# Recurrence gates as 64-row matmuls of two heads in turn, and the convolution and split of u by halves of the tokens

## The chip, the core and the metric

The kernel runs on one core of one Trainium2 chip. Its engines, as the profile names them, are PE (TensorE: matmuls, with their weight loads shown apart as PEld), DVE (VectorE), ACT (ScalarE), POOL (GpSimd) and SP (SyncE, which issues the DMAs). Each runs its own instructions in order and waits on semaphores for the others. The metric is device time in microseconds (us) for one execution of the whole kernel, as a median over executions.

## The reference, cut to what matters

One encoder block on x of 1024 tokens by 1024 channels, in float32. A combined projection gives u, a gate g, attention inputs q, k, v and two merge gates. The change touches the recurrent mixer only:

```
uc = centred_depthwise_conv(u, conv_w, conv_b)        # 4 taps over tokens: t-2 .. t+1
h_fwd = rg_lru(uc, lam[0], wa[0], ba[0], wx[0], bx[0], False)
h_bwd = rg_lru(uc, lam[1], wa[1], ba[1], wx[1], bx[1], True)
y_a = (h_fwd + h_bwd) * gelu(g)

def rg_lru(u, lam, wa, ba, wx, bx, reverse):
    ub = u.reshape(bsz, s, 16, 64)                    # 16 heads of 64 channels
    r = sigmoid(einsum("bshi,hij->bshj", ub, wa) + ba)
    i = sigmoid(einsum("bshi,hij->bshj", ub, wx) + bx)
    log_a = -8 * r * softplus(-lam)
    a = exp(log_a);  beta = sqrt(max(-expm1(2 * log_a), 0))
    h = scan(h[t] = a[t] * h[t-1] + beta[t] * i[t] * u[t])   # over the tokens
```

`wa` and `wx` are 64x64 for each head and direction. Windowed attention (mixer B), the merge sigmoid(zA) * y_a + sigmoid(zB) * y_b, the product with w_out, and a SwiGLU follow; the change leaves them alone.

## The kernel before, in words

**Layout and precision.** Channels lie on the 128 partitions and the 1024 tokens along the row. Each float32 operand of a product is split into a high and a low part of TensorE's 32-bit matmul type: a copy to the rounded type (`to_hi`) and a subtraction (`to_lo`, L127). Each product then takes three matmuls: high x high, high weight x low data, low weight x high data. `xh`, `xl` are the normalised x; `whi`, `wlo` a weight block of 1024 rows by 128 columns, in a ring of three; their raw block `wraw` comes by DMA into a ring of two.

**Stages.** The kernel starts up, runs attention (to about 404 us), then a loop over eight chunks c = 0 to 7 of 128 channels for the recurrence (to about 690 us), then the product with w_out (`wo`) in two halves, then the SwiGLU.

**One chunk of the recurrence.** `token_product` makes the products u, g and za (the merge gate), each 48 matmuls: two halves n of 512 tokens, eight blocks k of the contraction, three matmuls for each. u goes into a PSUM tile `pu` of 1024 columns, of which there is one; g and za go through `pa`, two PSUM tiles of 512 columns in turn, which `evac_g` (gelu, into `gg`) and `evac_za` (tanh, into `sA`) empty on ScalarE. From the third chunk on the order is u, g, za; for the first two it is g0, za0, u0, g1, u1, za1.

When both halves of u are there, `evac_u` makes the convolution: one ScalarE operation over 1024 tokens (L599) and three on VectorE that add the other taps (L603), all reading `pu` and writing `uc`. Then `lru_chunk` is started. It fetches the heads' weights into `graw`, whose four 128x128 blocks (`wa`, `wx`, each for directions d = 0 and 1) hold two 64x64 heads on the diagonal and zeros elsewhere (L729 clears it once), splits them into `gh` (ScalarE) and `gl` (GpSimd), splits `uc` into `uh` (ScalarE, L120) and `ul` (VectorE, L127), and runs the gates: for each of four blocks a PSUM tile `gp` (two in turn), six matmuls, and one sigmoid of 128x1024 (L659) into `r` or `i`. Then come, for the two directions: tanh (L671) and a maximum (L672) into `q`, `i` times `uc` (L673), exp (L678), sqrt (L681), `q` times (1 + a) (L684), `i` times `q` (L685), and the scan (L687, L689). Their sum (L690) is multiplied by `gg` (L694) and added to the attention's result `y` (L695). ScalarE loads a table whenever it changes to a function of another set (the ACT_TABLE_LOAD rows).

**What sets the order.** TensorE's order is the order in which the code issues it. `clock` is a running estimate: `mm` adds 0.00042 us for each column, so 0.215 for 512. `lru_chunk` is a generator: each `yield` puts it into the heap `waiting` with a due time that many us ahead, and between two steps of the products `run_due` resumes what is due. So the numbers after `yield` place the four gate blocks between the projections' matmuls; `drain` at the end runs what is left. The other engines' order is chosen by the compiler's scheduler from its own estimates; `tc.high_priority` moves an operation ahead, `tc.issue_after(x)` keeps it behind x. Each engine then works strictly in that order. Buffers are rings too: `uc`, `gg` and `sA` share four (`qutile`), `uh` has two, `pu` one.

**Weights.** `weight(key)` hands out the block for a product and first fetches and splits all blocks up to two further along. `prep` says on which engine: GpSimd for both parts during the recurrence; ScalarE for the high part after `prep["hi"] = "act"`, which stands in front of the last `drain`. The first `wo` block is asked for at L861.

Of the kernel before, what the change touches and what calls it, by code (L numbers as in the profile page):

```python
# [16 lines left out]
P = 128  # L17
# [6 lines left out]
HD = 64  # L24
# [7 lines left out]
def kernel(  # L32
# [190 lines left out]
    def cb(c):  # L223
        return pv[:, 64 + c:65 + c]

    def gb(t, d, c):
        o = (88, 104)[t] + d * KD + c
        return pv[:, o:o + 1]

    stat = const.tile([P, 4 * NT], F32, name="stat")  # L230
    rstd = const.tile([P, 3 * NT], F32, name="rstd")
# [136 lines left out]

    def softplus():

        lam = pv[:, 72:88]
        e, z, z2, po = lt
        act.activation(e, lam, AF.Abs)
        act.activation(e, e, AF.Exp, scale=-1.0)
        dve.tensor_scalar(out=z, in0=e, scalar1=2.0, scalar2=None, op0=ALU.add)
        dve.reciprocal(z, z)
        dve.tensor_tensor(out=z, in0=z, in1=e, op=ALU.mult)
        dve.tensor_tensor(out=z2, in0=z, in1=z, op=ALU.mult)
        dve.tensor_scalar(out=po, in0=z2, scalar1=1.0 / 17.0, scalar2=None, op0=ALU.mult)
        for n in (15, 13, 11, 9, 7, 5, 3):  # L380
            dve.scalar_tensor_tensor(out=po, in0=po, scalar=1.0 / n, in1=z2, op0=ALU.add, op1=ALU.mult)
        dve.scalar_tensor_tensor(out=po, in0=po, scalar=1.0, in1=z, op0=ALU.add, op1=ALU.mult)
        dve.tensor_scalar(out=e, in0=lam, scalar1=-1.0, scalar2=0.0, op0=ALU.mult, op1=ALU.max)
        dve.scalar_tensor_tensor(out=e, in0=po, scalar=2.0, in1=e, op0=ALU.mult, op1=ALU.add)
        dve.tensor_scalar(out=sp4, in0=e, scalar1=0.5 * C_RG, scalar2=None, op0=ALU.mult)
        dve.tensor_scalar(out=spm8, in0=e, scalar1=-C_RG, scalar2=None, op0=ALU.mult)
# [204 lines left out]
    lru = {"open": False, "gates": 0, "done": 0, "mm": False}  # L591
    gs = {}

    def evac_u(c):

        ps = gs.pop(("u", c))
        uc = qutile("uc")
        with tc.high_priority():
            act.activation(uc, ps, AF.Identity, bias=cb(c), scale=cw(2, c))  # L599
            for k in (0, 1, 3):  # L600
                sh = k - 2
                lo, hi = max(0, -sh), min(S, S - sh)
                dve.scalar_tensor_tensor(out=uc[:, lo:hi], in0=ps[:, lo + sh:hi + sh], scalar=cw(k, c),  # L603
                                         in1=uc[:, lo:hi], op0=ALU.mult, op1=ALU.add)
        gs["uc", c] = uc

    def evac_g(c):
        def f(n, sl, ps):
            if n == 0:
                gs["g", c] = qutile("gg")  # L610
            with tc.high_priority():
                act.activation(gs["g", c][:, sl], ps, AF.Gelu_apprx_tanh)
        return f

    def evac_za(c):
        def f(n, sl, ps):
            if n == 0:
                gs["za", c] = qutile("sA")
            act.activation(gs["za", c][:, sl], ps, AF.Tanh, bias=hbg[:, c:c + 1], scale=0.5)
            if n == 1:  # L620
                g = gs["g", c]
                dve.scalar_tensor_tensor(out=g, in0=gs.pop(("za", c)), scalar=1.0, in1=g,
# [4 lines left out]
    def lru_chunk(p2, psB, graw, c):  # L627


        def t2(tag, bufs=1, dt=F32):  # L630
            return p2.tile([P, S], dt, name=tag, tag=tag, bufs=bufs)

        for t, w in ((0, lru_wa), (1, lru_wx)):
            for j in range(2):
                o = slice(j * HD, (j + 1) * HD)
                dma(graw[o, 2 * t:2 * t + 2, o], w[0, :, 2 * c + j].rearrange("d i o -> i d o"))
        gh = p2.tile([P, 4, P], F32R, name="gh", tag="gh", bufs=2)
        gl = p2.tile([P, 4, P], F32R, name="gl", tag="gl", bufs=2)
        to_hi("act", gh, graw)
        to_lo("pool", gl, graw, gh)  # L640
        uc = gs.pop(("uc", c))
        uh = t2("uh", 2, F32R)
        ul = kmtile("ul", F32R)
        with tc.high_priority():
            to_hi("act", uh, uc)
            to_lo("dve", ul, uc, uh)
        last = c == KD - 1
        yield 11.5 if last else 15.5
        gate = {}
        for t in range(2):  # L650
            for d in range(2):
                gp = psB.tile([P, S], F32, name="gp", tag="gp", bufs=2)
                for n in range(2):
                    sl = slice(n * 512, (n + 1) * 512)
                    mm(gp[:, sl], gh[:, 2 * t + d, :], uh[:, sl], True, False)
                    mm(gp[:, sl], gh[:, 2 * t + d, :], ul[:, sl], False, False)
                    mm(gp[:, sl], gl[:, 2 * t + d, :], uh[:, sl], False, True)
                r = t2("ri"[t], 3)
                sig = act.activation(r, gp, AF.Sigmoid, bias=gb(t, d, c)).ins  # L659
                gate[t, d] = r  # L660
                if (t, d) != (1, 1):
                    yield 1.5 if last else 2.0
        lru["gates"] += 1
        if last:
            while not lru["mm"]:
# [37 lines left out]
    def mixers():  # L703
# [19 lines left out]
        def switch():  # L723
            if env[0] is None and att["done"] == H and att["gated"] == 2 * KD:
                st1.close()
                p2 = st2.enter_context(tc.tile_pool(name="p2", bufs=1))
                psB = st2ps.enter_context(tc.tile_pool(name="ps2", bufs=1, space=PSUM))
                graw = p2.tile([P, 4, P], F32, name="graw")
                pool.memset(graw, 0.0)  # L729
                env[0] = (p2, psB, graw)  # L730

        def u_halves(c):
            ps = env[0][1].tile([P, S], F32, name="pu", tag="pu", bufs=1)
            for n in range(2):
                sl = slice(n * 512, (n + 1) * 512)
                yield from token_product(("u", c), sl, xh, xl, ps[:, sl])
            gs["u", c] = ps
            evac_u(c)
            spawn(lru_chunk(*env[0], c))

        for _ in project(("g", 0), xh, xl, evac_g(0)):
            switch()
# [16 lines left out]
        run_due()  # L759


    prep["hi"], prep["lo"] = "act", "pool"
    drain(lambda: lru["gates"] == KD)
    st2ps.close()
# [93 lines left out]
                load_residual(RESIDUAL_AT[n])  # L858
            yield

    weight(("wo", 0, 0))  # L861
    for c in range(4):
        merged_split(0, c)
    lru["mm"] = True
# [490 lines left out]
```

## Time and profile before

| | us |
|---|---|
| median of 3 runs (lowest, highest) | 1431.94 (1431.26, 1432.14) |
| the profiled execution | 1431.24 |
| its span in the trace | 1429.4 |
| recurrence, 404 to 690 in the trace: PE busy | 285.15 of 286.00 |
| the same: DVE, ACT, POOL busy | 206.81, 169.96, 105.97 |

The mean granted TensorE clock is 0.998 of full speed. A row of the trace gives the start (us from the span's start), the duration, the engine, the line, the operation, the output and inputs, the shapes, and in brackets the idle time ahead of it with what ended it. In a table of windows each engine's busy time in a stretch is followed by its number of instructions. In the grouped rows the figures after the bar are the group's busy time and the mean ns of one instruction, then the idle time ahead. Matmuls are pipelined, so their durations overlap; the distance from one start to the next is what one costs.

### The profile page before, as it was taken

How to read it: one execution, taken by the hardware profiler on the slowest of the kernel's cores; microseconds unless marked ns; L12 is line 12 of the kernel's file. 1: busy time of each engine (PE TensorE's matmuls, PEld its weight loads, DVE VectorE, ACT ScalarE, POOL GpSimd, SP SyncE). 2: the span in 40 equal slices, each digit the busy share in tenths (PEclk: the TensorE clock that was granted, in tenths of full speed). 3: DMA queues.
4: the chain of work that ended last, by engine and by line, in shares of the span. 5: the costliest groups of instructions: out<-in, count | busy, mean ns of one | idle time of the engine just before them, and what ended most of it. 6: DMA issues, size and time to landing. Idle time of an engine off the chain costs nothing.

```text
span 1429.4 us, 18414 instructions
## 1 busy us (share of the span) xinstructions
PE 1401.7 (98%) x6606; PEld 1167.0 (82%) x6606; DVE 933.1 (65%) x1429; ACT 689.8 (48%) x1259; POOL 566.1 (40%) x522
## 2 busy tenths in 40 slices
PE   7999999999999999999999999999999999999997
PEld 6888888888888888888788878888888888888886
DVE  6357776777525887777877865444445444897886
ACT  6346656556526855555544533333323332544446
POOL 3434454554442443333444334555555562110002
PEclk9999999999999999999999999999999999999999
DMA  5111100110121111111243333333334435957643
GB/s 193 45 45 30 30 20 27 30 31 15 31 56 49 36 46 49 49 44 44 75 161 119 103 111 108 99 115 106 119 118 133 125 106 187 336 180 233 204 139 140
DMA packets 147548, 138.90 MB, mean 97 GB/s; under 512 B 11528, under 2 KB 117120, under 8 KB 147456
## 3 DMA queue, kind: packets, MB, share of 16 engines
q1 hardware_dynamic: 147456, 137.72, 30.9%
q8 instruction: 52, 0.85, 0.2%
q14 instruction: 40, 0.33, 0.1%
HBM read 119.08 MB, written 18.61 MB: 96 GB/s over the span
## 4 chain that ended last, share of the span: by engine, by line
PE 48%; DVE 2%; ACT 1%; issue 0%; POOL 0%; ACTq 0%
PE wo L86 35%; PE pa L86 12%; PE wo L90 1%; DVE x L1256 0%; DVE wop L127 0%; DVE ho L1169 0%; ACT x L1279 0%; ACT ho L1169 0%; ACT sg L1260 0%; DVE x L1276 0%; DVE h L1169 0%; ACT x L1273 0%; ACT wop L981 0%; DVE wo L1169 0%; DVE H L1049 0%
## 5 line engine op out<-in xcount | busy, mean ns | idle before, releaser
L86 PE MATMUL wo<-x,wop 128*128 128x512 f32 x1368 | 320.7, 390 | 1.9 <-DVE u L1025 1.1
L86 PEld LDWEIGHTS wo<-x,wop 128*128 128x128 f32 x1368 | 255.5, 188 | 55.9 <-ACT wop L981 2.7
L86 PE MATMUL pa<-xh,whi 128*128 128x512 f32 (+1 forms) x576 | 226.6, 393 | 0.6 <-ACT xh L250 0.5
L86 PE MATMUL pa<-xl,whi 128*128 128x512 f32 (+1 forms) x576 | 224.8, 390 | 0.9 <-DVE xl L251 0.7
L86 PE MATMUL pa<-xh,wlo 128*128 128x512 f32 (+1 forms) x576 | 223.7, 388 | 0.0
L127 POOL TENSOR_TENSOR wlo<-wraw,whi 128x1024 fp32r<-128x1024 f32 (+1 forms) x60 | 160.4, 2674 | 53.8 <-ACT whi L120 50.3
L86 PE MATMUL wo<-wo,ho 128*128 128x512 f32 x726 | 170.3, 389 | 0.0
L86 PEld LDWEIGHTS wo<-wo,ho 128*128 128x128 f32 x726 | 136.2, 188 | 28.7 <-DVE ho L1169 0.4
L124 POOL TENSOR_SCALAR whi<-wraw 128x1024 fp32r<-128x1024 f32 (+1 forms) x47 | 56.4, 1200 | 204.8 <-PE pa L86 141.3
L86 PEld LDWEIGHTS pa<-xh,wlo 128*128 128x128 f32 x576 | 108.3, 188 | 23.1
L86 PEld LDWEIGHTS pa<-xl,whi 128*128 128x128 f32 x576 | 108.5, 188 | 16.9 <-DVE xl L251 2.1
L86 PEld LDWEIGHTS pa<-xh,whi 128*128 128x128 f32 x576 | 108.5, 188 | 16.1 <-ACT xh L250 0.8
L86 PE MATMUL pa<-x,wop 128*128 128x512 f32 x480 | 117.2, 391 | 0.0
L512 POOL TENSOR_SCALAR s<-s,es 128x384 f32<-128x384 f32 (+1 forms) x128 | 71.9, 580 | 97.2 <-DVE es L510 72.4
L572 DVE TENSOR_TENSOR pl<-pt,ph 128x384 fp32r<-128x384 f32 (+1 forms) x128 | 66.9, 522 | 60.5 <-ACT ph L571 57.7
L981 ACT ACTIVATE wop<-s 128x512 fp32r<-128x512 f32 x66 | 41.6, 630 | 130.1 <-POOL s L970 65.9
L86 PEld LDWEIGHTS pa<-x,wop 128*128 128x128 f32 x480 | 89.5, 188 | 18.0
L507 ACT ACTIVATE s<-s,nm 128x384 f32<-128x384 f32 (+1 forms) x128 | 74.0, 580 | 40.5 <-DVE nm L504 39.3
L571 ACT ACTIVATE ph<-pt 128x384 fp32r<-128x384 f32 (+1 forms) x128 | 58.6, 458 | 64.2 <-PE pt L90 49.6
L127 DVE TENSOR_TENSOR wop<-s,wop 128x512 fp32r<-128x512 f32 x66 | 53.0, 803 | 49.4 <-ACT wop L981 48.6
L498 DVE CUSTOM_DVE_ANT_0 s<-sp,bias 128x384 f32<-128x384 f32 (+1 forms) x128 | 66.3, 519 | 24.2 <-PE sp L86 22.9
L1262 POOL TENSOR_TENSOR x<-x,x 128x512 f32<-128x512 f32 x8 | 11.8, 1490 | 166.8 <-ACT sg L1260 166.8
(210 smaller groups left out, 2727.6 us busy)
## 6 DMA issues: line engine op xcount, KB each, us to landing
wraw<-in_w_in_dram SPq DMA_DIRECT2D x44, 512.0 KB, 3.9
wq<-in_w_ffn_out_dram SPq DMA_DIRECT2D x88, 256.0 KB, 3.8
wraw<-in_w_ffn_in_dram SPq DMA_DIRECT2D x26, 512.0 KB, 4.0
wup<-in_w_ffn_in_dram SPq DMA_DIRECT2D x22, 512.0 KB, 4.7
hid<-H SPq DMA_DIRECT2D x22, 512.0 KB, 3.2
h<-hid SPq DMA_DIRECT2D x44, 256.0 KB, 5.4
s<-in_w_ffn_out_dram SPq DMA_DIRECT2D x66, 128.0 KB, 2.2
wraw<-in_w_out_dram SPq DMA_DIRECT2D x16, 512.0 KB, 3.5
```

Of the source, the lines that this page charges most:

```text
L86: pe.matmul(o, lhsT, rhs, start=start, stop=stop, skip_group_check=True)
L90: pe.transpose(o, i, ident)
L124: pool.tensor_scalar(out=o, in0=i, scalar1=1.0, scalar2=1.0, op0=ALU.mult, op1=ALU.mult)
L127: (dve if eng == "dve" else pool).tensor_tensor(out=o, in0=i, in1=hi.bitcast(F32), op=ALU.subtract)
L498: dve.tensor_tensor_reduce(out=s[:, :n], in0=sp[:, :n], in1=bias[:, off:off + n], scale=1.0, scalar=-3.0e38, op0=ALU.add, op1=ALU.max, acc ...
L507: act.activation(s[:, :n], s[:, :n], AF.Exp, bias=nm[:, j:j + 1], accum_out=sm[:, j:j + 1])
L512: pool.tensor_scalar(out=s[:, :n], in0=s[:, :n], scalar1=es[:, j:j + 1], scalar2=1.0, op0=ALU.mult, op1=ALU.mult)
L571: act.activation(ph[:, o:o + n], pt[:, :n], AF.Copy)
L572: dve.tensor_tensor(out=pl[:, o:o + n], in0=pt[:, :n], in1=ph[:, o:o + n].bitcast(F32), op=ALU.subtract)
L981: act.activation(t[:, lo4], src, AF.Copy)
L1262: pool.tensor_tensor(out=x1[t][:, lo4], in0=x1[t][:, lo4], in1=gfin[:, lo4], op=ALU.mult)
```

## The change

**Gates by head.** `graw`, `gh` and `gl` shrink from four blocks to two, one for each direction. Head j (0 or 1) of the chunk lies on the partitions 64 j to 64 j + 63, and the 64 columns of `wa` stand beside the 64 of `wx`. The zeros and the memset go. For each direction there are two PSUM tiles `gp`, one for each head; a matmul reads 64 rows of the weight and of `uh` or `ul`, and the two heads alternate, so consecutive matmuls use different halves of the rows. Their number stays: 12 for each direction, 24 for a chunk. A head's tile holds r on 64 partitions and i on the other 64, so a direction takes four sigmoids of 64x1024, eight for a chunk instead of four of 128x1024. The biases are rearranged to match by three small copies in `softplus`. The gates now stand in two runs of 12 matmuls, the first for d = 0, instead of four runs of six, and the planner's `clock` gains 0.1 less for each of their matmuls.

**u by halves.** `conv` takes the place of `evac_u` and runs after each half of u, cut at token 511 because the last tap looks one token ahead. `lru_chunk` starts 3.0 us after the first half, splits that half, and later the second; the second split is placed 5.2 us further in the planner's clock, and each split is kept behind the latest evacuation of g or za (`last_evac`).

**Weights.** The request for the first `wo` block moves ahead of the change of `prep`, so the splits it triggers run on GpSimd.

The diff, without empty lines:

```diff
--- before.py
+++ after.py
@@ -223,9 +223,10 @@
     def cb(c):
         return pv[:, 64 + c:65 + c]
-    def gb(t, d, c):
-        o = (88, 104)[t] + d * KD + c
-        return pv[:, o:o + 1]
+    def gb(t, j, d, c):
+        o = 88 + j * 16 + d * KD + c
+        return pv[t * HD:(t + 1) * HD, o:o + 1]
     stat = const.tile([P, 4 * NT], F32, name="stat")
     rstd = const.tile([P, 3 * NT], F32, name="rstd")
@@ -368,6 +369,10 @@
     def softplus():
+        top, bottom = slice(0, HD), slice(HD, P)
+        dve.tensor_copy(lt[0][top, :], pv[bottom, 88:104])
+        dve.tensor_copy(pv[bottom, 88:104], pv[top, 104:120])
+        dve.tensor_copy(pv[top, 104:120], lt[0][top, :])
         lam = pv[:, 72:88]
         e, z, z2, po = lt
         act.activation(e, lam, AF.Abs)
@@ -591,32 +596,37 @@
     lru = {"open": False, "gates": 0, "done": 0, "mm": False}
     gs = {}
-    def evac_u(c):
-        ps = gs.pop(("u", c))
-        uc = qutile("uc")
+    CUT = 511
+    last_evac = [None]
+    def conv(c, n, ps):
+        if n == 0:
+            gs["uc", c] = qutile("uc")
+        uc = gs["uc", c]
+        a, b = (0, CUT) if n == 0 else (CUT, S)
         with tc.high_priority():
-            act.activation(uc, ps, AF.Identity, bias=cb(c), scale=cw(2, c))
+            act.activation(uc[:, a:b], ps[:, a:b], AF.Identity, bias=cb(c), scale=cw(2, c))
             for k in (0, 1, 3):
                 sh = k - 2
-                lo, hi = max(0, -sh), min(S, S - sh)
+                lo, hi = max(a, -sh), min(b, S - sh)
                 dve.scalar_tensor_tensor(out=uc[:, lo:hi], in0=ps[:, lo + sh:hi + sh], scalar=cw(k, c),
                                          in1=uc[:, lo:hi], op0=ALU.mult, op1=ALU.add)
-        gs["uc", c] = uc
     def evac_g(c):
         def f(n, sl, ps):
             if n == 0:
                 gs["g", c] = qutile("gg")
             with tc.high_priority():
-                act.activation(gs["g", c][:, sl], ps, AF.Gelu_apprx_tanh)
+                last_evac[0] = act.activation(gs["g", c][:, sl], ps, AF.Gelu_apprx_tanh).ins
         return f
     def evac_za(c):
         def f(n, sl, ps):
             if n == 0:
                 gs["za", c] = qutile("sA")
-            act.activation(gs["za", c][:, sl], ps, AF.Tanh, bias=hbg[:, c:c + 1], scale=0.5)
+            last_evac[0] = act.activation(gs["za", c][:, sl], ps, AF.Tanh, bias=hbg[:, c:c + 1], scale=0.5).ins
             if n == 1:
                 g = gs["g", c]
                 dve.scalar_tensor_tensor(out=g, in0=gs.pop(("za", c)), scalar=1.0, in1=g,
@@ -627,39 +637,51 @@
     def lru_chunk(p2, psB, graw, c):
         def t2(tag, bufs=1, dt=F32):
             return p2.tile([P, S], dt, name=tag, tag=tag, bufs=bufs)
         for t, w in ((0, lru_wa), (1, lru_wx)):
             for j in range(2):
                 o = slice(j * HD, (j + 1) * HD)
-                dma(graw[o, 2 * t:2 * t + 2, o], w[0, :, 2 * c + j].rearrange("d i o -> i d o"))
-        gh = p2.tile([P, 4, P], F32R, name="gh", tag="gh", bufs=2)
-        gl = p2.tile([P, 4, P], F32R, name="gl", tag="gl", bufs=2)
+                dma(graw[o, :, t * HD:(t + 1) * HD], w[0, :, 2 * c + j].rearrange("d i o -> i d o"))
+        gh = p2.tile([P, 2, P], F32R, name="gh", tag="gh", bufs=2)
+        gl = p2.tile([P, 2, P], F32R, name="gl", tag="gl", bufs=2)
         to_hi("act", gh, graw)
         to_lo("pool", gl, graw, gh)
-        uc = gs.pop(("uc", c))
+        uc = gs["uc", c]
         uh = t2("uh", 2, F32R)
         ul = kmtile("ul", F32R)
-        with tc.high_priority():
-            to_hi("act", uh, uc)
-            to_lo("dve", ul, uc, uh)
+        for n, o in enumerate((slice(0, CUT), slice(CUT, S))):
+            while n == 1 and ("u", c) not in gs:
+                yield 0.5
+            if n == 1:
+                yield 5.2
+            with tc.high_priority(), tc.issue_after(last_evac[0]):
+                to_hi("act", uh[:, o], uc[:, o])
+                to_lo("dve", ul[:, o], uc[:, o], uh[:, o])
+        del gs["uc", c], gs["u", c]
         last = c == KD - 1
-        yield 11.5 if last else 15.5
+        yield 5.0 if last else 10.0
         gate = {}
-        for t in range(2):
-            for d in range(2):
-                gp = psB.tile([P, S], F32, name="gp", tag="gp", bufs=2)
+        for d in range(2):
+            gp = [psB.tile([P, S], F32, name="gp", tag="gp", bufs=2) for _ in range(2)]
+            for g, m, st, sp in ((gh, uh, True, False), (gh, ul, False, False), (gl, uh, False, True)):
                 for n in range(2):
                     sl = slice(n * 512, (n + 1) * 512)
-                    mm(gp[:, sl], gh[:, 2 * t + d, :], uh[:, sl], True, False)
-                    mm(gp[:, sl], gh[:, 2 * t + d, :], ul[:, sl], False, False)
-                    mm(gp[:, sl], gl[:, 2 * t + d, :], uh[:, sl], False, True)
+                    for j in range(2):
+                        o = slice(j * HD, (j + 1) * HD)
+                        mm(gp[j][:, sl], g[o, d, :], m[o, sl], st, sp)
+                        clock[0] -= 0.1
+            for t in range(2):
                 r = t2("ri"[t], 3)
-                sig = act.activation(r, gp, AF.Sigmoid, bias=gb(t, d, c)).ins
+                i = slice(t * HD, (t + 1) * HD)
+                for j in range(2):
+                    o = slice(j * HD, (j + 1) * HD)
+                    sig = act.activation(r[o, :], gp[j][i, :], AF.Sigmoid, bias=gb(t, j, d, c)).ins
                 gate[t, d] = r
-                if (t, d) != (1, 1):
-                    yield 1.5 if last else 2.0
+            if d == 0:
+                yield 4.5 if last else 5.5
         lru["gates"] += 1
         if last:
             while not lru["mm"]:
@@ -725,8 +747,7 @@
                 st1.close()
                 p2 = st2.enter_context(tc.tile_pool(name="p2", bufs=1))
                 psB = st2ps.enter_context(tc.tile_pool(name="ps2", bufs=1, space=PSUM))
-                graw = p2.tile([P, 4, P], F32, name="graw")
-                pool.memset(graw, 0.0)
+                graw = p2.tile([P, 2, P], F32, name="graw")
                 env[0] = (p2, psB, graw)
         def u_halves(c):
@@ -734,9 +755,10 @@
             for n in range(2):
                 sl = slice(n * 512, (n + 1) * 512)
                 yield from token_product(("u", c), sl, xh, xl, ps[:, sl])
-            gs["u", c] = ps
-            evac_u(c)
-            spawn(lru_chunk(*env[0], c))
+                conv(c, n, ps)
+                if n == 0:
+                    spawn(lru_chunk(*env[0], c), 3.0)
+            gs["u", c] = True
         for _ in project(("g", 0), xh, xl, evac_g(0)):
             switch()
@@ -759,6 +781,7 @@
         run_due()
+    weight(("wo", 0, 0))
     prep["hi"], prep["lo"] = "act", "pool"
     drain(lambda: lru["gates"] == KD)
     st2ps.close()
@@ -858,7 +881,6 @@
                 load_residual(RESIDUAL_AT[n])
             yield
-    weight(("wo", 0, 0))
     for c in range(4):
         merged_split(0, c)
     lru["mm"] = True
```

How instructions stand on the engines, in three places. The names are those of the tiles; "x2" is a row that occurs twice in turn.

TensorE, in the last chunk, after g (c = 7). Before, six gate matmuls (`gp`) stood behind nine matmuls of za (`pa`):

```order
L86 MATMUL pa<-xh_97,whi 128x512
L86 MATMUL pa<-xl_105,whi 128x512
L86 MATMUL pa<-xh_97,wlo 128x512
L86 MATMUL gp<-uh,gh 128x512
L86 MATMUL gp<-ul,gh 128x512
L86 MATMUL gp<-uh,gl 128x512
L86 MATMUL gp<-uh,gh 128x512
L86 MATMUL gp<-ul,gh 128x512
L86 MATMUL gp<-uh,gl 128x512
L86 MATMUL pa<-xh_98,whi 128x512
```

After, still TensorE in the last chunk, from the first matmuls of za:

```order
L86 MATMUL pa<-xh_95,whi 128x512
L86 MATMUL pa<-xl_103,whi 128x512
L86 MATMUL pa<-xh_95,wlo 128x512
L86 MATMUL pa<-xh_96,whi 128x512
L86 MATMUL pa<-xl_104,whi 128x512
L86 MATMUL pa<-xh_96,wlo 128x512
L86 MATMUL gp<-uh,gh 128x512 x4
L86 MATMUL gp<-ul,gh 128x512 x4
L86 MATMUL gp<-uh,gl 128x512 x4
L86 MATMUL pa<-xh_97,whi 128x512
```

The first gates moved from behind nine matmuls of za to behind six, and come in a run of twelve, which reads both halves of `uh` and `ul`; the four runs of six became two, the second behind three matmuls of za's second half.

VectorE, in one of the middle chunks, from the first product behind the sqrt (L684 before, L706 after). Before (L603 is the convolution, L127 the low split of `uc`, L687 and L689 the scans):

```order
L684 SCALAR_TENSOR_TENSOR q<-r,q 128x1024
L603 SCALAR_TENSOR_TENSOR uc<-pu,pv,uc 128x1022
L685 TENSOR_TENSOR i<-i,q 128x1024
L603 SCALAR_TENSOR_TENSOR uc<-pu,pv,uc 128x1023
L687 SCALAR_TENSOR_TENSOR q<-r,i 128x1024
L603 SCALAR_TENSOR_TENSOR uc<-pu,pv,uc 128x1023
L684 SCALAR_TENSOR_TENSOR q<-r,q 128x1024
L127 TENSOR_TENSOR ul<-uc,uh 128x1024
L685 TENSOR_TENSOR i<-i,q 128x1024
L689 SCALAR_TENSOR_TENSOR q<-r,i 128x1024
L690 TENSOR_TENSOR q<-q 128x1024
```

After (L614 is the convolution, L709 and L711 the scans):

```order
L127 TENSOR_TENSOR ul<-uc,uh 128x511
L706 SCALAR_TENSOR_TENSOR q<-r,q 128x1024 x2
L707 TENSOR_TENSOR i<-i,q 128x1024 x2
L614 SCALAR_TENSOR_TENSOR uc<-pu,pv,uc 128x513
L709 SCALAR_TENSOR_TENSOR q<-r,i 128x1024
L614 SCALAR_TENSOR_TENSOR uc<-pu,pv,uc 128x513
L711 SCALAR_TENSOR_TENSOR q<-r,i 128x1024
L614 SCALAR_TENSOR_TENSOR uc<-pu,pv,uc 128x512
L712 TENSOR_TENSOR q<-q 128x1024
L716 TENSOR_TENSOR gg<-gg,q 128x1024
L127 TENSOR_TENSOR ul<-uc,uh 128x513
```

The low split of `uc` moved from between the products of the second direction to behind both scans, the sum and the product with `gg` for its second half; the first half's stands ahead of the four products.

ScalarE, in the third chunk (c = 2), from the convolution's operation to the first gelu (`gg`). Before:

```order
L599 ACTIVATE uc<-pu,pv 128x1024
L120 ACTIVATE gh<-graw 128x512
L659 ACTIVATE i<-gp,pv 128x1024
L678 ACT_TABLE_LOAD
L678 ACTIVATE r<-r,spm_87 128x1024
L120 ACTIVATE uh<-uc 128x1024
L612 ACT_TABLE_LOAD
L612 ACTIVATE gg<-pa 128x512
```

After (L610 is the convolution, L681 the sigmoid, L693 the tanh, L700 the exp, L622 the gelu):

```order
L610 ACTIVATE uc<-pu,pv 128x511
L693 ACTIVATE q<-r,sp_86 128x1024
L120 ACTIVATE uh<-uc 128x511
L610 ACTIVATE uc<-pu,pv 128x513
L120 ACTIVATE gh<-graw 128x256
L681 ACTIVATE r<-gp,pv 64x1024 x2
L681 ACTIVATE i<-gp,pv 64x1024 x2
L693 ACTIVATE q<-r,sp_86 128x1024
L700 ACT_TABLE_LOAD
L700 ACTIVATE r<-r,spm_87 128x1024
L622 ACT_TABLE_LOAD
L622 ACTIVATE gg<-pa 128x512
```

The split `uh` moved ahead: its first half now stands in front of the second half of the convolution, the sigmoids, the tanh and the gelu, where it stood behind the sigmoids and the first exp.

## The prediction

> **What bounds the kernel now.** First the page's totals, then the table of windows for one stretch of the recurrence stage, then the list of what TensorE waited for.
>
> ```profile
> PE 1401.7 (98%) x6606; PEld 1167.0 (82%) x6606; DVE 933.1 (65%) x1429; ACT 689.8 (48%) x1259; POOL 566.1 (40%) x522
> core 0: us, PE busy (x) PEld busy (x) DVE busy (x) ACT busy (x) POOL busy (x), PEclk, DMA share, GB/s
> 510.00:550.00 40.00, 40.00 (x178) 33.14 (x177) 30.05 (x20) 21.29 (x22) 16.27 (x8) 1.00 0.16 44
> PE pa L86 <- ACT sA L619: 0.8, 1, 0.8
> ```
>
> TensorE is never free in that stretch, and in the whole stage it waits once, 0.8 us. So only fewer or cheaper matmuls can shorten the stage, and only while the others keep up: VectorE is already busy 30 us of 40, ScalarE 21.
>
> **What the gates cost, and what pairing saves.** The grouped rows of the gate matmuls, two starts of a run of them with the next other matmul, then two weight loads from the start of the kernel:
>
> ```profile
> L86 PE MATMUL gp<-ul,gh 128*128 128x512 f32 x64 | 25.0, 391 | 0.0
> L86 PE MATMUL gp<-uh,gl 128*128 128x512 f32 x64 | 24.9, 389 | 0.0
> L86 PE MATMUL gp<-uh,gh 128*128 128x512 f32 x64 | 24.9, 389 | 0.0
> 525.10 0.39 PE L86 MATMUL gp<-uh,gh 128*128 128x512 f32 x1
> 525.33 0.39 PE L86 MATMUL gp<-ul,gh 128*128 128x512 f32 x1
> 526.46 0.39 PE L86 MATMUL pa<-xh,whi 128*128 128x512 f32 x1
> 20.26 0.19 PEld L86 LDWEIGHTS pa<-xl,whi 128*128 128x128 f32 x1
> 20.37 0.19 PEld L86 LDWEIGHTS pa<-xh,wlo 128*128 128x128 f32 x1
> ```
>
> The durations overlap; the step counts: six gate matmuls from 525.10 to 526.46, 0.227 us each. 3 x 64 of them take 43.5 us. The change keeps 192, but neighbours sit on different halves of the rows. No row shows a matmul on 64 rows. One bound is that each still takes 0.227: nothing saved. The other is that two run in one step: 21.8 us saved. Loads can start 0.11 us apart, so two fit into a step, and I take 21.8 (2.72 per chunk of 128 channels, 1.36 per run of twelve). Each of the 16 runs also goes into and out of the 64-row form; the nearest price is the part of a matmul past its step, 0.39 - 0.227 = 0.16 us, so 0 to 32 x 0.16 = 5.2 us. I take 0, because the next load already runs beside the current matmul in these rows; the 5.2 stays in the range.
>
> The Trainium skill, page "TensorE: Matmul & The Clock Gate", Part 3 (Packing small matmuls), says matmuls on different row groups start about 4 ns apart, and gives 3.07 times the speed for four. No run here shows it yet. If two keep the same share of their ideal, an estimate is 1.53 times, 15 us saved instead of 21.8. "TensorEngine Tiling (Array Packing)", Key Properties, adds that a change of mode drains TensorE, which speaks for the 5.2.
>
> **What ScalarE gains in work.**
>
> ```profile
> L659 ACT ACTIVATE r<-gp,pv x16: 1101/1117/1122, 434.2 to 677.8; 128x1024 f32<-128x1024 f32 x16
> 397.44 0.59 ACT L546 ACTIVATE tmp<-yp 64x512 f32<-64x512 f32 x1 [2.28 <-PE yp L86]
> 513.06 0.60 ACT L612 ACTIVATE gg<-pa 128x512 f32<-128x512 f32 x1 [2.92 <-PE pa L86]
> ```
>
> 64 partitions cost what 128 do (0.59 against 0.60 us for 512 columns), so eight sigmoids of 64x1024 for four of 128x1024 add about 4.4 us a chunk. The halved conv and split add some 0.1 us for each extra instruction; the smaller `gh`, `gl` save 0.2 and 0.6; the three copies in `softplus` and the dropped memset lie beside busy TensorE. Hidden or not, these count only through the chain below.
>
> **The chain that TensorE will wait for.** One period of ScalarE, VectorE and GpSimd around the u product that began at 531.90 and ended at 545.5:
>
> ```profile
> 539.26 1.10 ACT L659 ACTIVATE i<-gp,pv 128x1024 f32<-128x1024 f32 x1
> 540.38 1.28 ACT L678 ACT_TABLE_LOAD   x1
> 541.67 2.19 ACT L678 ACTIVATE r<-r,spm 128x1024 f32<-128x1024 f32 x2
> 543.88 1.28 ACT L681 ACT_TABLE_LOAD   x1
> 545.18 1.06 ACT L681 ACTIVATE q<-q 128x1024 f32<-128x1024 f32 x1
> 546.14 1.19 ACT L599 ACTIVATE uc<-pu,pv 128x1024 f32<-128x1024 f32 x1
> 555.66 1.06 ACT L120 ACTIVATE uh<-uc 128x1024 fp32r<-128x1024 f32 x1 [3.92 <-DVE uc L603]
> 531.90 0.39 PE L86 MATMUL pu<-xh,whi 128*128 128x512 f32 x1
> 546.27 1.38 DVE L684 SCALAR_TENSOR_TENSOR q<-r,q 128x1024 f32<-128x1024 f32 x1 [4.46 <-ACT q L681]
> 552.12 2.27 DVE L687 TENSOR_TENSOR_SCAN q<-r,i 128x1024 f32<-128x1024 f32 x1
> 554.32 1.25 DVE L603 SCALAR_TENSOR_TENSOR uc<-pu,pv,uc 128x1023 f32<-128x1023 f32 x1
> 556.76 1.93 DVE L127 TENSOR_TENSOR ul<-uc,uh 128x1024 fp32r<-128x1024 f32 x1
> 558.61 3.41 DVE L685 TENSOR_TENSOR i<-i,q 128x1024 f32<-128x1024 f32 x1
> 557.70 3.24 POOL L127 TENSOR_TENSOR wlo<-wraw,whi 128x1024 fp32r<-128x1024 f32 x1
> 672.66 0.39 PE L86 MATMUL gp<-uh,gh 128*128 128x512 f32 x1
> 670.99 1.93 DVE L127 TENSOR_TENSOR ul<-uc,uh 128x1024 fp32r<-128x1024 f32 x1
> ```
>
> Two things are read here. `ul`, which the gates need, was ready at 558.69, 13.2 us after the end of u; it stood ahead of one product and the second scan on VectorE. And VectorE's SBUF operations wait while GpSimd subtracts: the product at 558.61 took 3.41 us, of which 2.3 until the subtraction ended at 560.94; the conv, which reads PSUM, did not.
>
> Now the steady chunk in the changed order, in us from the first matmul of u. TensorE without waits: d=1 gates of the previous chunk 2.04 to 3.40, u done 12.24, g 23.12, first half of za 28.56, d=0 gates 29.92, end 35.36 (38.08 before). ScalarE: four sigmoids to 7.8, half conv 8.4, tanh 9.5, table 10.8, two exps 13.0, half split 13.5, table 14.8, first sqrt 15.85. VectorE starts behind the first `ul` half, which a subtraction of GpSimd holds to 16.45: four operations of 1.15 to 21.05, conv piece 21.7, scan 23.9, piece 24.55, GpSimd's copy until 24.95, scan 27.15, last piece 27.8. Only then can the second `uh` half run, to 28.4, and the second `gg`, which stands behind it on ScalarE, to 28.95: za's second half, due at 28.56, starts about 0.45 late. On VectorE the subtraction for the next u holds the sum to 30.6, then gg's product 31.8, then `ul` 32.45; the gates want it at 30.8, 1.65 late. So 2.1 us a chunk comes back. Chunks 3 to 6: **8.4 us** (nothing where VectorE wins the port).
>
> **The third chunk (c=2).**
>
> ```profile
> 453.63 2.01 ACT L681 ACTIVATE q<-q 128x1024 f32<-128x1024 f32 x2
> 478.63 0.60 ACT L612 ACTIVATE gg<-pa 128x512 f32<-128x512 f32 x1
> 480.22 0.39 PE L86 MATMUL pa<-xh,whi 128*128 128x512 f32 x1
> ```
>
> Before, the first `gg` of c=2 ended 1.0 us ahead of the za matmul that needs its bank (480.22). The change brings that matmul 4 x 1.36 us forward, to 474.8. On ScalarE the half `uh` stands ahead of everything to that `gg`, and waits for three conv pieces that VectorE has between older work. From the sqrts (455.6): four operations to 460, two scans to 464, copy of GpSimd 465, gg product 466, subtraction 468.3, sum, product, conv, product, conv, sum, conv to 475. Then half split, half conv, `gh`, four sigmoids, tanh, table, exp, table, `gg`: 11 us, 486. TensorE is 11.2 late, or 7.9 if VectorE keeps the port (3.3 less). I take 9.5, and 2.5 more in the next two gate runs and chunk 3, since ScalarE is still some 2 us behind there: **12.0 us**.
>
> **The last chunk (c=7).** Its gates stand right behind g and six matmuls, 24.5 us after u began, and want `ul` at 24.95. Before, they started at 672.66 and `ul` was ready at 672.92, just in time. Now the same VectorE order gives 32.45: **7.5 us**, and at least 4.8 with a free port. Behind it the wait for `sA` (0.8 above) grows with three more sigmoids; I add 0.7 (0 to 2). The early fetch of `wo` moves two splits from ScalarE to GpSimd, beside busy TensorE.
>
> **Sum.** -21.8 + 8.4 + 12.0 + 7.5 + 0.7 = +6.8 us. The profiled execution took 1431.24 us (its span 1429.4 and 1.8 around it), 0.7 below the median. 1431.24 + 6.8 = 1438.0; I forecast **1438**, the median as likely a little above.
>
> **Rivals.**
> *VectorE wins the port (faster).* The place is the moment when the subtraction for the next weights and VectorE's next operation both wait. If VectorE goes first at the four places above, chunks 3 to 6 wait for nothing, c=2 costs 7.9 + 0.5, c=7 4.8: -21.8 + 13.9 + 0.7 = -7.2, so 1424. It decides from 2 us a chunk; the rows show the loss at 558.61, but the subtraction then waited 1 us itself.
> *No pairing.* Each matmul takes 0.227 as before. The chain of some 29 us from the d=1 gates to `ul` still has to fit: chunks 3 to 6 take 40.7 instead of 38.1, c=2 is 6 late, c=7 6.5: +23, 1454. That is also the rival in which the change does not do what it says.
> *A slow restart.* After its first waits TensorE is slow:
>
> ```profile
> 10.68 0.58 PE L86 MATMUL pa<-xl,whi 128*128 128x256 f32 x1
> 15.79 0.28 PE L86 MATMUL pa<-xh,wlo 128*128 128x256 f32 x1
> ```
>
> 0.58 us for what takes 0.28 later, with 1.00 as granted clock in that window. If the waits of 9.5 and 7.5 us bring that back, at up to 2 us each, the time is 1442. The Trainium skill, "TensorE: Matmul & The Clock Gate", Part 1, names such a rule: after an idle window of about 3.4 us TensorE runs at half clock until it has been busy as long. By that rule this rival holds for c=2 at least; the first rows agree.
>
> **Chances.** Forecast (1433 to 1441) 0.38; VectorE wins (1420 to 1430) 0.30; slow restart 0.15; no pairing 0.12; 0.05 for other outcomes. A measurement can tell about 0.2% (2.9 us) from no change: 1429.1 to 1434.8. Of the second, 0.28 is faster; of the first, 0.12 lies in that band, with 0.03 from the second and the rest. Faster 0.30, same 0.15, slower 0.55. The range for 8 in 10: 1419 (all of the second case) to 1449 (half-way into no pairing).
>
> **What would show it.** Right: gate matmuls in pairs 0.227 us apart; a TensorE wait of 7 to 11 us on the first `gg` of c=2; one on `uh` and `ul` of c=7; about 2 us a chunk between; a span of 37.5 us a chunk. Wrong: gate matmuls one by one at 0.227; no wait on `gg`; `ul`'s second half ready within 18 us of u's end; subtractions of GpSimd that stretch past 5 us beside unstretched scans.

## The result and the profile after

The changed kernel takes 1491.3 us (median; 1489.5 to 1492.1) against 1432.0 for the kernel before, a ratio of 1.041 (1.0395 to 1.0431): 59 us slower. The forecast was 1438, range 1419 to 1449.

First the page of the changed kernel: the totals, and PE and its granted clock in 40 slices of the span.

```profile
PE 1408.3 (95%) x6606; PEld 1159.4 (78%) x6606; DVE 946.3 (64%) x1464; ACT 727.4 (49%) x1305; POOL 567.1 (38%) x522
PE   7999999999986978889999999999999999999997
PEclk9999999999988999999999999999999999999999
```

Apart from the first and the last slice, the digits below 9 lie in the recurrence (404 to about 747 us here), and the clock drops there too. The list of what TensorE waited for in the changed kernel (total us, times, longest), in its lines for the recurrence and the product behind it, names the cause; `mm` is the merged result, scaled and split, that the product with w_out reads:

```profile
PE pu L86 <- DVE uc L614: 50.5, 8, 14.3
PE pa L86 <- DVE mm L800: 2.2, 2, 1.5
PE pa L86 <- ACT sA L629: 1.4, 1, 1.4
PE gp L86 <- DVE ul L127: 0.4, 1, 0.4
```

Eight waits, one a chunk, each in the middle of u for its own convolution. No wait for `gg` is in the list, and nearly none for `ul`. One of the eight, in the timeline of a steady chunk:

```profile
616.65 0.39 PE L86 MATMUL pu<-xh,wlo 128*128 128x512 f32 x1
622.12 0.77 PE L86 MATMUL pu<-xh,whi 128*128 128x512 f32 x1 [5.09 <-DVE uc L614]
615.74 2.23 ACT L681 ACTIVATE i<-gp,pv 64x1024 f32<-64x1024 f32 x2
618.00 0.78 ACT L610 ACTIVATE uc<-pu,pv 128x511 f32<-128x511 f32 x1
618.00 1.23 DVE L695 TENSOR_TENSOR i<-i,uc 128x1024 f32<-128x1024 f32 x1 [1.74 <-ACT i L681]
619.15 0.74 DVE L614 SCALAR_TENSOR_TENSOR uc<-pu,pv,uc 128x509 f32<-128x509 f32 x1
619.84 0.69 DVE L694 TENSOR_SCALAR q<-q 128x1024 f32<-128x1024 f32 x1
620.45 1.53 DVE L614 SCALAR_TENSOR_TENSOR uc<-pu,pv,uc 128x510 f32<-128x510 f32 x2
```

The first half of u ends with the matmul at 616.65. The second half starts only at 622.12, when the last convolution piece of the first half has ended (620.45 + 1.53 = 621.98). That piece reads columns 1 to 511 of `pu`; the second half writes columns 512 to 1023. Ahead of the convolution stand two sigmoids on ScalarE, and on VectorE a product ahead of its pieces and a maximum among them. The stretches of that chunk before, during and after the restart, in the table of windows:

```profile
core 0: us, PE busy (x) PEld busy (x) DVE busy (x) ACT busy (x) POOL busy (x), PEclk, DMA share, GB/s
609.40:622.00 12.60, 7.63 (x38) 5.48 (x36) 10.12 (x8) 11.21 (x12) 5.98 (x3) 0.94 0.19 52
622.00:627.30 5.30, 5.18 (x12) 4.13 (x13) 1.76 (x2) 5.12 (x6) 0.00 (x0) 0.50 0.01 3
627.30:653.40 26.10, 26.10 (x120) 21.06 (x119) 18.64 (x13) 9.64 (x11) 10.12 (x4) 1.00 0.14 41
```

After the wait the granted clock is 0.50 for twelve matmuls: they take 5.2 us instead of 12 x 0.227 = 2.7, so the 5.1 us wait costs 7.6. Matmuls at this lower clock behind a wait are called a slow start below. Over the eight chunks the slow starts of u's second half add 17.2 us.

The gates themselves, one run of twelve:

```profile
611.44 0.39 PE L86 MATMUL pu<-xh,wlo 128*128 128x512 f32 x1
611.76 0.73 PE L86 MATMUL gp<-uh,gh 64*128 64x512 f32 x4
612.33 0.63 PE L86 MATMUL gp<-ul,gh 64*128 64x512 f32 x4
612.79 0.62 PE L86 MATMUL gp<-uh,gl 64*128 64x512 f32 x4
613.35 0.50 PE L86 MATMUL pu<-xh,whi 128*128 128x512 f32 x1
613.68 0.40 PE L86 MATMUL pu<-xl,whi 128*128 128x512 f32 x1
```

Two ordinary starts are 0.227 us apart. From 611.44 to 613.68 are 2.24 us; less two ordinary steps (0.45) the run costs 1.79, where 12 x 0.227 = 2.72 before. Of that, 1.36 is six paired steps and 0.43 is what entering, leaving and the first pair cost. The saving is 0.93 to 0.94 a run, 15.0 us for 16 runs.

The account: -15.0 for the gates, +50.5 of waits, +17.2 of slow starts, +2.0 in two gate runs that fell into such a slow stretch, +2.2 for `mm` and about 1 in the last chunk: +58, of 60.6 in the spans (1490.0 - 1429.4).

### The profile page after: what moved, and what is told of

Its sections match the earlier page's. It is cut to its first block, busy times and chain, and to the rows that moved or that the text cites. A ratio compares the mean times of both kernels' runs of the same rounds, so it can differ in the third digit from the quotient of the medians.

```text
span 1490.0 us, 18494 instructions
## 1 busy us (share of the span) xinstructions
PE 1408.3 (95%) x6606; PEld 1159.4 (78%) x6606; DVE 946.3 (64%) x1464; ACT 727.4 (49%) x1305; POOL 567.1 (38%) x522
## 4 chain that ended last, share of the span: by engine, by line
PE 76%; DVE 12%; ACT 8%; issue 2%; DMA 1%; SPq 0%; POOL 0%; ACTq 0%; DVEq 0%; POOLq 0%
PE wo L86 32%; PE pa L86 30%; PE pu L86 5%; PE yp L86 3%; PE sp L86 2%; PE pt L90 2%; DVE uc L614 1%; ACT i L681 1%; ACT r L681 1%; PE gp L86 1%; DVE q L711 1%; DVE i L707 1%; DVE i L695 1%; PE wo L90 1%; ACT s L512 1%
## 5 line engine op out<-in xcount | busy, mean ns | idle before, releaser
L127 POOL TENSOR_TENSOR wlo<-wraw,whi 128x1024 fp32r<-128x1024 f32 (+1 forms) x60 | 160.4, 2675 | 42.7 <-ACT whi L120 39.1
L86 PEld LDWEIGHTS pa<-xl,whi 128*128 128x128 f32 x576 | 108.7, 189 | 16.6 <-DVE xl L252 2.3
L86 PE MATMUL pu<-xh,whi 128*128 128x512 f32 x128 | 58.8, 460 | 50.5 <-DVE uc L614 50.5
L127 DVE TENSOR_TENSOR wop<-s,wop 128x512 fp32r<-128x512 f32 x66 | 53.5, 811 | 49.5 <-ACT wop L1003 48.6
```

Source lines behind the costliest of these rows:

```text
L86: pe.matmul(o, lhsT, rhs, start=start, stop=stop, skip_group_check=True)
L127: (dve if eng == "dve" else pool).tensor_tensor(out=o, in0=i, in1=hi.bitcast(F32), op=ALU.subtract)
```

## The experiments

Theory **one tile**: the second half of u waits for the first half's convolution only because both lie in one PSUM tile. By this theory the waits that the scheduler writes into the program for such a tile are kept for the tile as a whole: a write into it stands behind earlier reads of it, though they touch other columns. Rivals: the wait is for the work itself (**late convolution**), or the 64-row matmuls bring the loss (**gates cost**).

Three runs set these against each other, and a fourth asks what pairing is worth.

**two_tiles.** u in two tiles of 512 columns. The cut below shows the tiles; `conv` changes with them, since the values that a tap takes across the boundary go through a small buffer, with two short VectorE operations more in each half:

```diff
-            ps = env[0][1].tile([P, S], F32, name="pu", tag="pu", bufs=1)
+            ps = []
             for n in range(2):
...
+                ps.append(env[0][1].tile([P, 512], F32, name="pu", tag="pu", bufs=2))
-                yield from token_product(("u", c), sl, xh, xl, ps[:, sl])
+                yield from token_product(("u", c), sl, xh, xl, ps[n])
```

> The halves of u go into two PSUM tiles of 512 columns instead of one of 1024; the few values that a tap takes across the boundary (3 for a channel) are kept aside by small VectorE operations. All else as in the changed kernel. Theory ONE TILE: the second half of u waits for the first half's convolution only because both lie in one tile; with two tiles the 50.5 us of these waits and the 17.2 us of slow matmuls behind them go, so 1491 - 68 = 1423 if nothing else comes; the waits of the recorded forecast for gg and ul (up to 28.6 us) can come in part, so 1417 to 1446. Theory LATE CONVOLUTION (the wait is for the work on ScalarE and VectorE, whatever the tile): waits of 3 to 5 us a chunk stay, 1475 or more.

1431.4 us, ratio 0.9993 (0.9984 to 1.0003). The compiled program shows it already. The first matmul of u's second half, in the changed kernel (where it waits for the first half's operations on both engines) and with two tiles:

```
L86 MATMUL pu<-xh_95,whi 128x512 [waits DVE_49,Activation_49]
L86 MATMUL pu<-xh_95,whi 128x512
```

In the trace of two_tiles the waits on `uc` are gone, the steady chunk takes 36.2 us at full clock, and others appear (a window of one chunk, then lines of TensorE's list):

```profile
573.00:609.20 36.20, 36.20 (x169) 28.95 (x168) 31.27 (x26) 25.83 (x28) 17.45 (x7) 1.00 0.17 48
PE pa L86 <- ACT gg L635: 6.9, 1, 6.9
PE pa L86 <- DVE mm L814: 2.2, 2, 1.5
PE pa L86 <- ACT sA L642: 1.5, 1, 1.5
...
PE gp L86 <- ACT i L694: 0.9, 1, 0.9
```

36.2 is 38.08 less two runs' 0.94. No wait of 3 to 5 us a chunk is left, as late convolution would have it, and 59.9 us are gone: one tile is the cause of the loss. What pairing saves is then given back elsewhere, mostly to the first `gg` of the third chunk: 6.9 us and some 1.6 of slow start behind it.

**gates_only.** Gates by head; `evac_u` and the whole split as before the change. The early request for `wo` stays, here and in halves_only.

> The gates by head alone; convolution and split of u whole, as before the change. Theory ONE TILE: no wait in the middle of u; 16 runs of twelve gate matmuls at 1.79 us instead of 2.73 save 15.0 us, so 1417, and up to 1425 with small new waits. Theory GATES COST (the 64-row matmuls themselves bring the loss, by draining TensorE or by eight sigmoids instead of four): 1440 or more.

1431.9 us, ratio 1.0002 (0.9993 to 1.0011). Gate runs take 1.79 us here too, and 64-row matmuls bring no loss where nothing is late, but 1417 was missed. From TensorE's list:

```profile
PE pa L86 <- ACT gg L620: 3.2, 1, 3.2
PE gp L86 <- DVE ul L127: 2.6, 1, 2.6
```

The same `gg`, and `ul` in the last chunk, whose run of gates takes 5.8 us instead of 1.8. This profile also starts the recurrence 2.3 us later than that of the kernel before, which has to do with the stages ahead of it. With the slow starts and two waits for `mm` (2.2 us) these come to some 15 of the 16.4 us that are missing in the spans (1430.8 where 1429.4 - 15.0 would be 1414.4).

**halves_only.** Halves of u in one tile; gates on 128 rows in four runs of six.

> The convolution and split of u by halves alone, in one PSUM tile; gates on 128 rows in four runs of six, as before. Theory ONE TILE: each chunk's second half of u waits 3 to 6 us for the first half's convolution and restarts slowly (2.5 us), 45 to 70 us in all, so 1475 to 1505. Theory GATES COST: no such loss, about 1432.

1496.2 us, ratio 1.0448 (1.0433 to 1.0463). The loss comes with the halves alone:

```profile
PE pu L86 <- DVE uc L609: 47.0, 8, 11.8
```

**heads_in_blocks.** Per direction the six matmuls of head 0, then those of head 1.

```diff
-                for n in range(2):
-                    sl = slice(n * 512, (n + 1) * 512)
-                    for j in range(2):
+            for j in range(2):
+                o = slice(j * HD, (j + 1) * HD)
+                for g, m, st, sp in ((gh, uh, True, False), (gh, ul, False, False), (gl, uh, False, True)):
```

> As the changed kernel, but the six matmuls of head 0 stand ahead of the six of head 1, so neighbours use the same half of the rows. If the saving comes from pairing, a run of twelve takes 2.7 us or more instead of 1.6 from its first start to the next other matmul, and the time grows by 15 us, to 1506 (less where the waits for the convolution shrink). If 64-row matmuls are cheaper by themselves, the run stays at 1.6 us and the time at 1491.

1498.1 us, ratio 1.0462 (1.0447 to 1.0476): 6.8 us over the changed kernel, not 15. A run takes 2.36 us, between 1.79 and 2.72. The timeline of this kernel says why:

```profile
605.39 0.73 PE L86 MATMUL gp<-uh,gh 64*128 64x512 f32 x2
605.96 0.39 PE L86 MATMUL gp<-ul,gh 64*128 64x512 f32 x1
605.97 0.49 PE L86 MATMUL gp<-uh,gh 64*128 64x512 f32 x1
606.20 0.39 PE L86 MATMUL gp<-ul,gh 64*128 64x512 f32 x1
```

A second `uh,gh` starts 0.01 us behind a `ul,gh`, though in the program all three products of a head precede the other head's: matmuls of the two halves of the rows overlap even where they aren't neighbours. Alternating is still worth 0.57 us a run. 16 runs of that are 9.1 us; against it the waits in the middle of u come to 46.7 us here, 3.8 less than in the changed kernel.

Where do the 15 us go in two_tiles? On ScalarE, ahead of the third chunk's first `gg`:

```profile
477.52 0.63 ACT L120 ACTIVATE uh<-uc 128x511 fp32r<-128x511 f32 x1 [4.52 <-DVE uc L612]
478.18 2.23 ACT L694 ACTIVATE i<-gp,pv 64x1024 f32<-64x1024 f32 x2
...
481.61 1.28 ACT L713 ACT_TABLE_LOAD   x1
482.90 1.15 ACT L713 ACTIVATE r<-r,spm 128x1024 f32<-128x1024 f32 x1
484.07 1.28 ACT L635 ACT_TABLE_LOAD   x1
485.36 0.60 ACT L635 ACTIVATE gg<-pa 128x512 f32<-128x512 f32 x1
```

ScalarE stands idle for 4.5 us, until the first half of `uc` is ready for the split, while the sigmoids, an exp and the gelu queue behind it. The next runs try to take that away, and the wait for `mm` with it.

**two_tiles_wo_late.** two_tiles with `weight(("wo", 0, 0))` at its old place.

> Two tiles for u, and the request for the first wo block back at its old place. In two_tiles TensorE waits 2.2 us for mm in the product with w_out (and restarts 0.2 us late), which the kernel before doesn't. Theory EARLY WO (the splits moved to GpSimd hold VectorE): these waits go, 1429. Theory SHORTER LEAD (the last chunk's work on VectorE is as late as before, and TensorE arrives 3 us earlier): they stay, 1431.

1435.6 us, ratio 1.0023 (1.0013 to 1.0033): 4.2 us slower than two_tiles, so both theories fall. One wait for `mm` of 4.6 us and a slow start of 2.8 us behind it take the place of two short ones. The split that fell to ScalarE again, then `mm` for chunk 4 in this kernel, then the same `mm` in two_tiles:

```profile
686.24 1.05 ACT L120 ACTIVATE whi<-wraw 128x1024 fp32r<-128x1024 f32 x1
709.75 2.76 DVE L813 SCALAR_TENSOR_TENSOR mm<-y,mm 128x512 fp32r<-128x512 f32 x1
```

```profile
708.30 0.66 DVE L814 SCALAR_TENSOR_TENSOR mm<-y,mm 128x512 fp32r<-128x512 f32 x1
```

The last chunk's exps, square roots and scans follow 1.4 us later, and `mm` then takes 2.76 us instead of 0.66. The early request is worth some 4 us here.

**two_tiles_g2_first, g2_first_early_merge, g2_first_wo_late_early_merge.** The third chunk's g ahead of its u; then also `merged_split` for six chunks instead of four ahead of `lru["mm"] = True`; then also the late request.

```diff
...
+            if c == 2:
+                yield from project(("g", c), xh, xl, evac_g(c))
             yield from u_halves(c)
-            yield from project(("g", c), xh, xl, evac_g(c))
+            if c != 2:
+                yield from project(("g", c), xh, xl, evac_g(c))
```

> Two tiles for u, and in the third chunk g stands ahead of u, so its first gelu doesn't queue behind the split of u, the sigmoids and an exp on ScalarE. Theory: of the 15.0 us that pairing saves, 6.9 + 1.6 us went into the wait for that gelu and the slow restart; without it 1431.4 - 8.5 = 1423. Rival (the backlog of the second chunk only moves to another wait of the third): 1428 or more.

> As two_tiles_g2_first, and the scaled splits of merged chunks 4 and 5 are issued ahead of the last chunk's recurrence instead of behind it. If the 2.2 us of waits for mm come from VectorE's order, they go: 2.5 us less than two_tiles_g2_first, about 1420.5. If the splits of chunks 6 and 7 become late instead, no gain.

> As g2_first_early_merge, with the request for the first wo block at its old place. Theory EARLY WO: up to 1 us faster than g2_first_early_merge. Theory SHORTER LEAD: the same within 1 us.

1448.1, 1447.4 and 1448.6 us (ratios 1.011, 1.0106 and 1.0116, each within 0.002): 16 to 17 us slower than two_tiles. The wait moved, as the rival said, and grew. From TensorE's list of two_tiles_g2_first:

```profile
PE gp L86 <- ACT i L694: 11.5, 7, 6.3
PE pa L86 <- ACT sA L642: 8.4, 2, 6.9
```

It waits for `sA` of the second chunk and for the sigmoids, which must give `gp` free. That the early merge takes the wait for `mm` away can be read from its list, not from these times. The late request gained nothing in the third: 1.2 us slower than the second, where theory early wo had it up to 1 us faster.

**two_tiles_early_merge, third_split_later, third_split_exp_later.** two_tiles with the six early merges; then both splits of the third chunk issued behind its first `gg`, with the gates' delay behind them shortened; then the second chunk's exps behind that `gg` too.

```diff
+        while c == 2 and ("g", c) not in gs:
+            yield 0.3
         for n, o in enumerate((slice(0, CUT), slice(CUT, S))):
...
-                yield 5.2
+                yield 0.3 if c == 2 else 5.2
...
-        yield 5.0 if last else 10.0
+        yield 5.0 if last else 4.0 if c == 2 else 10.0
```

> Two tiles for u, and the scaled splits of merged chunks 4 and 5 issued ahead of the last chunk's recurrence. The 2.2 us of waits for mm and their 0.2 us of slow restart go: 1431.4 - 2.4 = 1429. If chunks 6 and 7 become late instead, 1431 or more.

> As two_tiles_early_merge, and in the third chunk both splits of u are issued behind its first gelu. On ScalarE the split waited 4.5 us for the convolution in front of two sigmoids, a tanh, an exp and that gelu, for which TensorE waited 6.9 us. Theory QUEUE (ScalarE waits in order): the wait for the gelu shrinks to about 2.4 us and brings no slow restart (1.6 us), so 1429 - 6 = 1423. Rival BACKLOG (the work behind it is as late anyway): a wait of similar size for the third chunk's gates, 1428 or more.

> As third_split_later, and the second chunk's two exps are issued behind the third chunk's first gelu too. Theory QUEUE: the remaining wait of some 2.4 us for that gelu goes as well, 1421. Rival BACKLOG: exps, square roots and the next gates are later by as much, no gain over third_split_later.

1430.6 (0.9989, 0.998 to 0.9998), 1429.9 (0.9985, 0.9976 to 0.9994) and 1431.0 us (0.9991, 0.9982 to 1.0). The first gains less than the 2.4 us expected and can hardly be told from two_tiles. In the second the wait for `gg` shrank from 6.9 to 2.4 us as expected, but the time didn't follow. From its list:

```profile
PE pa L86 <- ACT gg L635: 2.4, 1, 2.4
PE gp L86 <- DVE ul L127: 2.0, 1, 2.0
```

The shortened delay had put the third chunk's first gates at 483.05, against 494.58 in two_tiles_early_merge, ahead of the `ul` they read. So this run couldn't tell queue from backlog. The third gained nothing, as backlog had it, but it kept these early gates (2.9 us of wait for `ul`), and its wait for `gg` stayed at 2.4 us though both exps now stand behind that gelu. Something else holds the gelu; the row of its table load in third_split_exp_later names it:

```profile
479.97 1.28 ACT L635 ACT_TABLE_LOAD   x1 [3.17 <-DVE y L734]
```

L734 adds the product with `gg` to `y`. In the compiled program the gelu of the third chunk writes the buffer of the first chunk's `gg`, which that operation still reads. So what is left of the wait is one for a free buffer, and moving exps can't shorten it; no run tried one buffer more. One more run put the gates back:

**third_gates_back.** third_split_later with `yield 10.0` for the third chunk, as for the others.

> As third_split_later, but the third chunk's first gates stay 10.0 instead of 4.0 us of the planner's clock behind the second split, where two_tiles_early_merge has them. In third_split_later the wait for the gelu shrank to 2.4 us as theory QUEUE says, but the gates were placed 10 us earlier and their run took 5.9 us instead of 1.8, and 3.0 us more went to a slow restart. Theory QUEUE: with the gates back both go: two_tiles_early_merge's 1430.6 less 4.5 us of wait and 1.6 us of slow restart, 1424.5. Rival BACKLOG: the third chunk's work is late wherever the gates stand, 1429 or more.

1425.3 us (1424.7 to 1425.8), ratio 0.9953 (0.994 to 0.9967): faster than the kernel before by 6.4 us and than the changed one by 66. Theory queue holds: 1424.5 was expected. From TensorE's list, and a steady chunk's window:

```profile
PE pa L86 <- ACT gg L635: 2.4, 1, 2.4
PE gp L86 <- ACT i L696: 1.8, 3, 0.9
567.90:604.10 36.20, 36.20 (x169) 28.95 (x168) 31.26 (x26) 25.82 (x28) 17.44 (x7) 1.00 0.17 48
```

## Why the prediction was wrong, point by point

**The step that failed** stands in the steady chunk: "TensorE without waits: d=1 gates of the previous chunk 2.04 to 3.40, u done 12.24". I let u run through its middle, and took from the halved convolution only that work comes earlier. I followed the order of the instructions on each engine, and for TensorE asked only about the reads of `gp`, `gg`, `uh` and `ul`. That a half-read tile is written again I never asked, and so put this wait at nothing, though the matmul's two waits stand in the compiled program, as shown above. two_tiles and halves_only show the step: with one tile 47.0 to 50.5 us of waits, with two none. None of my rivals held it. That the forecast was slower, too, is luck: of the waits that made its sum positive, on `gg` and `ul`, the changed kernel shows 0.4 us.

**The slow restart** was a rival at 0.15, priced "up to 2 us each" for two waits. It came at once behind seven of the eight waits, at 1.7 to 2.8 us each, 17.2 in all. The granted clock is 0.50 there, where the rows of the kernel's start that I took as agreeing had 1.00. What a wait costs isn't set by its length alone: halves_only lost 2.9 us behind a wait of 3.31 us and nothing behind one of 3.37, and in the changed kernel the same 3.37 us at 441.64 brought the slow clock only 1.7 us later, into the next run of gates. The Trainium skill, "TensorE: Matmul & The Clock Gate", Part 1, says that the clock falls after an idle window of about 3.4 us, and that the window runs freely. The runs agree with a window that doesn't begin with the wait, but not that it takes 3.4 us of idling. In third_split_later a shorter wait was enough:

```profile
481.66 0.60 PE L86 MATMUL pa<-xh,whi 128*128 128x512 f32 x1 [2.45 <-ACT gg L635]
```

The granted clock is 0.58 in the 1.45 us behind it and 0.50 in the 5 us after that, while 2.41 us in third_gates_back left it at 1.00.

**Pairing** was right in kind. Forecast 21.8 with up to 5.2 for going in and out: measured 15.0, a little under the lower end of 16.6. "I take 0, because the next load already runs beside the current matmul" was the mis-sized term: it is 0.43 us a run, 6.8 in all. The estimate from the Trainium skill, "TensorE: Matmul & The Clock Gate", Part 3, was 15 us and came out, but by luck: it took each pair as slower than two to one, while here the pairs run at two to one and the loss lies at the ends of the run.

**Steady chunks, 8.4 us, and the last chunk, 7.5.** Neither came. In the changed kernel TensorE was late itself, and the last chunk's wait for `ul` was 0.4 us. In two_tiles a steady chunk has no wait at all and the last none for `ul`; there the second half of `ul` is done at 561.0, 11.6 us behind the end of u at 549.4, where I had it 20 us behind. But in two_tiles that split stands ahead of both scans on VectorE, and I had added up the order of the changed kernel, which has it behind the scans, their sum and the product with `gg`. So no run shows what this term would have been in that order without the big wait. The rows of two_tiles:

```profile
549.41 0.39 PE L86 MATMUL pa<-xh,whi 128*128 128x512 f32 x1
560.35 0.69 DVE L127 TENSOR_TENSOR ul<-uc,uh 128x513 fp32r<-128x513 f32 x1
560.32 3.76 POOL L124 TENSOR_SCALAR whi<-wraw 128x1024 fp32r<-128x1024 f32 x1 [7.35 <-PE pa L86]
573.01 1.05 POOL L124 TENSOR_SCALAR whi<-wraw 128x1024 fp32r<-128x1024 f32 x1 [4.60 <-PE pa L86]
```

The last two rows bear on the rival in which VectorE wins the port: beside `ul` and the first scan GpSimd's copy took 3.76 us instead of 1.05, so here GpSimd stood back. In the steady chunk I had let VectorE wait at every meeting. Nor does VectorE always win: a few us later its sum at 566.25 took 3.25 us beside a subtraction that had begun at 564.17, where the same sum took 1.21 in the last chunk of two_tiles_wo_late. In the sum for that rival I counted the 0.7 for `sA` twice: 7.9 + 0.5 + 4.8 is 13.2, not 13.9, which makes it 1423 instead of 1424. The gates_only run, with the old split, did wait for `ul` in the last chunk, 4.0 us.

**The third chunk, 12.0 us.** In the changed kernel it didn't come: TensorE had stood for 14.3 us in the middle of that chunk's u. Right in its place and mechanism once that wait is gone: in two_tiles 6.9 us on the first `gg` (forecast 9.5) and 1.6 of slow start, and third_gates_back gains 5.3 us on two_tiles_early_merge by taking the split out of ScalarE's way.

**The end.** `sA` grew by 0.6, as forecast (0.7). The early `wo`, which I had put beside busy TensorE at no gain, saves some 4 us in two_tiles.

## What to carry to other kernels

Cutting work into halves lets it start earlier only if the producer may go on: where a consumer reads the first half of a PSUM tile, look at the waits of the matmul that writes the second half, or give each half its own tile. The lower clock behind the waits added a third to them here (17.2 us on 50.5), so one short stall a loop turn can outweigh what the change saves. And when work on the bounding engine gets cheaper, look for the next instruction that was only just in time: here it was one gelu behind a split that waited in ScalarE's queue.

## What the runs showed of the hardware that was not expected

Matmuls on the two halves of the rows overlap even when six of one stand ahead of six of the other: 2.36 us for twelve instead of 2.72. Going into and out of such a run costs 0.43 us with the first pair. A wait of 3.3 us can be followed by 2.9 us lost to the half clock, or by none, and one of 2.45 us was enough to bring it. In SBUF the changed kernel's compiled program does tell columns apart: ScalarE's convolution of the second half writes `uc` without a wait for VectorE's split, which reads the first half. Left open: whether the waits in PSUM follow the tile or another unit coarser than its columns; only one and two tiles were tried.
